# Layer 0's mix: products with h in plain fp32, four column blocks accumulated at once over all K, and no weight splits on GpSimd

## The chip, the core and the metric

The kernel runs on one NeuronCore of a Trainium2 chip. TensorE (PE in the profile) does matrix products into PSUM, VectorE (DVE) and ScalarE (ACT) do elementwise work, GpSimd (POOL) does elementwise work in SBUF, and SyncE (SP) issues DMA transfers from HBM. Each engine works through its own queue in order; semaphores join them. The metric is the device time of one execution in microseconds (us).

## What is computed

The reference is a two-layer decoder trunk for 256 tokens of width 2048, in float32. Only layer 0's mix is touched by the change:

```python
mod = cond @ w_ada[layer] + b_ada[layer]          # six vectors of 2048 for each layer
h = rmsnorm(x, g_pre_mix[layer]) * (1 + sc_m) + sh_m
z = h @ w_in_ab[i]                                # 2048 -> 5408 columns
y_a = chunked_spatial_gating(z[..., :2 * A_WIDTH], ...)
y_b = rwkv7_time_mix(z[..., 2 * A_WIDTH:], ...)
y = jnp.concatenate([y_a, y_b], axis=-1) @ w_out_ab[i]
x = x + gt_m * rmsnorm(y, g_post_mix[layer])
```

Behind it come layer 0's SwiGLU FFN, layer 1's attention, and layer 1's FFN. The conditioning matrix `w_ada` is 201 MB in all; shift and scale of layer 0's mix (33.5 MB of it) are needed before h exists, the other ten vectors are needed later.

## The kernel before, in words

**Products.** Every large product goes through the same scheme. Activations lie transposed in SBUF, 16 K-tiles of 128 rows by 256 tokens. A chunk is a weight tile of 256 rows of K by 512 columns (512 KB), loaded by SP into `w32` (four buffers). `load_split` (L187) makes two fp32r tiles of it: `wh`, a rounded copy by ACT (L193), and `wl`, the remainder `w32 - wh`, by DVE or, every `Split.every`-th time, by GpSimd (L194 to L196). The activation is split the same way, into h and l. A product of one K-tile and one token tile is then three fp32r matmuls, h wh + h wl + l wh (`mm_chunk`, L207 to L209). `dense` (L221) runs one block of 512 columns over all of K in two PSUM banks of the pool `ps_mm` (four banks; the pool `ps_ms` has the other four, for everything small).

**Start of layer 0.** `strips(kt)` (L425) loads two 1 MB strips of `w_ada` into four slots, takes their dot products with the conditioning vector on DVE (`ada_dot`, L115), and makes K-tile kt of h: `h32` on DVE (L437), its rounded copy `H0` on ACT (L438) and the remainder `L0` on DVE (L439). Since K-tiles become ready one by one, the first seven column blocks (`first`: lora of 288 columns, then k0, k1, r0, r1, v0, v1 of 512) are run in four groups of four K-tiles. For each group and block, two PSUM banks are filled with four K-tiles (`group_block` and `mm_group`, L456 to L458) and added to an SBUF tile (`acc`: a copy by ACT for the first group at L464, an add by DVE at L466 after that).

**The background program.** `rk_gen` (L502 to L902) is the RWKV-7 part: token shift, decay, keys, scores of 64-token chunks, inverses of triangular blocks (L670 to L719, mostly DVE), the chain over four chunks (L721 to L890, small fp32 matmuls), group norm and `YB`. It is a generator that yields a cost at each step. After each weight chunk `pump` (L164) adds credit (`Bg.rate`, 1.8 a chunk and 3 from the chain on) and takes steps of it for that credit. The yields add up to about 121: lora and decay 14.3, keys 17.9, r, bonus and v 16, scores 8, inverses 31.8, chain and norms 33. It waits for blocks that are not yet in the set `have`. `pump` also takes steps of `ada_gen` (L118), each a 512 KB load of `w_ada` and a dot product on DVE; its rate is 1 a chunk, and 2.2 from the chain on.

**Order of layer 0.** First the four groups, where the background program runs beside the last (`last_group`, L910, 14 chunks); then four `dense` blocks of the gMLP part (`evac_av` and `evac_au`, 32 chunks); then the half of w_out that reads `YA` (L994, 16 chunks), with what is left of the background program; then the half that reads `YB` (L1024, 16 chunks), and `residual_norm`. A scheduler of the framework orders instructions within the queues, so that neighbouring steps may change places.

Of the kernel before, what the change touches and what calls it, by code (L numbers as in the profile page):

```python
# [14 lines left out]
P = 128  # L15
# [7 lines left out]
GROUPS = (4, 4, 4, 4)  # L23
# [29 lines left out]
def trunk(ctx: ExitStack, tc, io, out, dbg=None):  # L53
# [12 lines left out]

    cols = cpool.tile([P, NCOL], F32, name="cols")
# [31 lines left out]
    cond = cpool.tile([P, D], F32, name="cond")  # L99
    A.dma_start(cond, io["c"].to_broadcast([P, D]))  # L100
# [82 lines left out]
    class Split:  # L183
        n = 0
        every = 0

    def load_split(src, ncol):  # L187
        w32 = wpool.tile([P, 2, 512], F32, tag="w32", name="w32", bufs=4)
        SY.dma_start(w32[:, :, :ncol], src)  # L189
        wh = wpool.tile([P, 2, 512], F32R, tag="wh", name="wh", bufs=3)  # L190
        wl = wpool.tile([P, 2, 512], F32R, tag="wl", name="wl", bufs=3)
        with tc.high_priority(PRI):
            A.activation(wh[:, :, :ncol], w32[:, :, :ncol], AF.Copy)  # L193
            Split.n += 1  # L194
            eng = G if Split.every and Split.n % Split.every == 0 else V
            eng.tensor_sub(wl[:, :, :ncol], w32[:, :, :ncol], wh[:, :, :ncol].bitcast(F32))  # L196
        return wh, wl
# [13 lines left out]
    class Late:  # L211
        """steps of an evacuation that wait for the next block's first chunks"""
# [73 lines left out]
    def residual_norm(X, U, st, layer, which, Ht, Lt, base=None):  # L286
# [4 lines left out]
        # mean (x + r u)^2 from the sums, then its root  # L291
# [77 lines left out]
    # =================== layer 0 mix ===================  # L369
    xT = hpool.tile([P, KT, S], F32, tag="X", name="xT")  # L370
    A.dma_start(xT, io["xT"])
    H0 = new_hT("H0", "hT0")
    L0 = new_hT("H1", "hT0l")
    hx, lx = hl(H0, L0)

# [16 lines left out]
    slots = [KBf[:, 0:D], KBf[:, D:2 * D], SCf[:, 0:D], SCf[:, D:2 * D]]  # L392
# [3 lines left out]
    vAf = vA.rearrange("p t n -> p (t n)")  # L396

# [12 lines left out]
    with tc.tile_pool(name="spool", bufs=1) as sp:  # L410
        # 1 / rms of every token, on all partitions
        sq = RA.rearrange("p x g s -> p (x g) s")
# [8 lines left out]
        V.reciprocal(rbc, rbc)  # L421

        ns = [0]

        def strips(kt):  # L425
            cc = sp.tile([P, 2], F32, tag="cc", name="cc", bufs=3)
            for s_ in range(2):
                w = slots[ns[0] % 4]
                ns[0] += 1
                SY.dma_start(w, io["w_ada"][0, s_, kt])  # L430
                ada_dot(w, 0, D, cc[:, s_:s_ + 1])
            V.tensor_add(cc[:, 0:1], cc[:, 0:1], col("b_ada", kt))
            V.tensor_scalar(cc[:, 1:2], cc[:, 1:2], col("b_ada", KT + kt), 1.0, op0=OP.add,
                            op1=OP.add)
            V.tensor_mul(cc[:, 1:2], cc[:, 1:2], col("g_pre_mix", kt))
            h32 = sp.tile([P, S], F32, tag="h32", name="h32", bufs=2)
            V.scalar_tensor_tensor(h32, xT[:, kt, :], cc[:, 1:2], rbc, op0=OP.mult, op1=OP.mult)  # L437
            A.activation(H0[:, kt, :], h32, AF.Identity, bias=cc[:, 0:1])  # L438
            V.scalar_tensor_tensor(L0[:, kt, :], h32, cc[:, 0:1], H0[:, kt, :].bitcast(F32),  # L439
                                   op0=OP.add, op1=OP.subtract)  # L440

        def group_block(src, ncol, k0, n):
            ps = [ps_mm.tile([P, 512], F32, name="mm") for _ in range(NT)]
            for c in range(n // 2):
                wh, wl = load_split(src(k0 // 2 + c), ncol)
                mm_group(ps, c, k0, wh, wl, ncol, n)
                yield ps

        def mm_group(ps, c, k0, wh, wl, ncol, n):
            for k in range(2):  # L450
                j = 2 * c + k
                kt = k0 + j
                for t in range(NT):
                    o = ps[t][:, :ncol]
                    h, l = hx(kt, t), lx(kt, t)
                    T.matmul(o, h, wh[:, k, :ncol], start=(j == 0), stop=False)  # L456
                    T.matmul(o, h, wl[:, k, :ncol], start=False, stop=False)  # L457
                    T.matmul(o, l, wh[:, k, :ncol], start=False, stop=(j == n - 1))  # L458

        def acc(nm, ps, ncol, gi):  # L460
            z = zn_tiles[nm]
            for t in range(NT):
                if gi == 0:
                    A.activation(z[:, t, :ncol], ps[t][:, :ncol], AF.Copy)  # L464
                else:
                    V.tensor_tensor(z[:, t, :ncol], z[:, t, :ncol], ps[t][:, :ncol], op=OP.add)  # L466

        Split.every = 3
        k0 = 0
        for kt in range(GROUPS[0]):  # L470
            strips(kt)
        nk = GROUPS[0]
        for gi, n in enumerate(GROUPS[:-1]):
            nxt = GROUPS[gi + 1]
            done, slot, total = 0, 0, len(first) * n // 2
            for nm, src, ncol in first:
                for ps in group_block(src, ncol, k0, n):
                    slot += 1
                    while done < nxt and done * total < slot * nxt:
                        strips(nk)  # L480
                        nk += 1
                        done += 1
                acc(nm, ps, ncol, gi)
            k0 += n
    dump("h", H0)
    A.dma_start(indT, io["indT"])

    def head_bcast(out, g, rows):
        """rows of heads 2g, 2g+1 onto their 64 partitions each"""
        T.matmul(out, indT[:, g, :], rows, start=True, stop=True)  # L490
# [3 lines left out]
    E = hpool.tile([P, 2, 8, S], F32, tag="X", name="E")  # L494
    have = set()
# [6 lines left out]
    def rk_gen():  # L502
        # lora
# [78 lines left out]
        # kk  # L582
# [22 lines left out]
        # k' and b  # L605
# [31 lines left out]
        # causal scores of every chunk: strict against the removal keys, full against r  # L637
        Bg.rate = 1.8
        SRA = hpool.tile([P, 64, 64], F32, tag="X", name="SRA")
# [29 lines left out]
        # inverse of the 32 x 32 diagonal blocks  # L669
        Ada.rate, Split.every = 1, 2  # L670
# [50 lines left out]
        # chain over the chunks  # L721
        Bg.rate = 3
        Ada.rate, Split.every = 2.2, 3
# [63 lines left out]
        def group_norm(ts, gw):  # L787
            """y = (y - mean) rstd G1 + B1 for a range of tokens, gw pairs of heads at a time"""
# [106 lines left out]
        YB = hpool.tile([P, 2, 8, S], F32R, tag="X", name="YB")  # L895
# [12 lines left out]
    Split.every = 2  # L908

    def last_group():  # L910
        n = GROUPS[-1]
        k0 = KT - n
        for nm, src, ncol in first:
            for ps in group_block(src, ncol, k0, n):
                pump(AR, BR)
            acc(nm, ps, ncol, len(GROUPS) - 1)
            have.add(nm)

    last_group()
# [6 lines left out]
    # A: gelu, layernorm of v  # L926
# [6 lines left out]
    for b in range(2):  # L933
        dense(lambda ch, b=b: win[6 + b, ch], KT, hx, lx, 512, evac_av(b), AR, BR)
# [37 lines left out]
    for b in range(2):  # L972
        dense(lambda ch, b=b: win[8 + b, ch], KT, hx, lx, 512, evac_au(b), AR, BR)
    YA = hpool.tile([P, 2, 8, S], F32R, tag="H1", name="YA")
# [27 lines left out]
    Split.every = 3  # L1002
# [28 lines left out]
    Split.every = 0  # L1031
# [4 lines left out]
    # =================== FFN ===================  # L1036
# [53 lines left out]
    # =================== layer 1 attention ===================  # L1090
# [117 lines left out]
def _layout(inputs):  # L1208
# [24 lines left out]
    def tiled(w, cols_list):  # L1233
        """[K, N] -> [blocks, K/256, 128, 2, width]"""
# [70 lines left out]
```

## Time and profile before

| | us |
|---|---|
| median of 3 runs (lowest, highest) | 2599.43 (2598.14, 2600.51) |
| the profiled execution, span | 2604.5 |
| layer 0's mix in it, to the last product with YB | 641.7 |
| PE busy, whole span | 2415.6 |
| DVE busy, whole span | 1770.2 |
| POOL busy, whole span | 235.9 |

The profiled execution is the only one with a trace, and its span is its own time; it is 5.1 us (0.2%) longer than the median. In the views by stretch, each row gives a stretch of the span, the busy time of each engine with its number of instructions, the granted TensorE clock as a share of full speed, the busy share of the DMA engines, and the bytes that they moved. A busy time joins instructions that overlap.

### The profile page before, as it was taken

The page shows a single profiled execution, that of the slowest core. Times are in us where ns is not written, and L with a number is a line of the kernel's source. Part 1 is how long each engine was busy: PE and PEld are TensorE (multiplying, and loading weights), DVE is VectorE, ACT ScalarE, POOL GpSimd, SP SyncE. Part 2 cuts the span into 40 slices and gives each one's busy share as a digit, 9 for nine tenths or more (in the row PEclk, how much of TensorE's full clock was granted, in tenths as well). Part 3 has the DMA queues.
Part 4 walks back from the last instruction along what each step waited for, and adds up shares of the span by engine and source line. Part 5 has one row for each costly group of instructions (what it writes and reads, how often), then busy time and mean ns, then how long its engine had stood idle before and what let it go on. Part 6 is the DMA issues. An engine that isn't in the chain of part 4 may idle for free. (4 is left out here: it accounts for less than half of the span.)

```text
span 2604.5 us, 30648 instructions
## 1 busy us (share of the span) xinstructions
PE 2415.6 (93%) x11296; PEld 1944.2 (75%) x11296; DVE 1770.2 (68%) x2318; ACT 1115.7 (43%) x1508; POOL 235.9 (9%) x131
## 2 busy tenths in 40 slices
PE   4888887997999999999998999999999999999998
PEld 3666666855778777788887777877777888888886
DVE  6998999468777777754545788786777545444444
ACT  3436332435544434444444444445644444443443
POOL 1222752002100000000000010000100000000000
PEclk8999898879999999999999999999999999999999
DMA  9867665458689888755555788886587555556554
GB/s 364 323 256 271 207 211 202 155 163 287 212 308 318 311 299 303 276 190 204 192 194 170 251 306 307 298 305 237 180 312 279 191 187 191 187 188 209 192 190 152
DMA packets 167126, 623.55 MB, mean 239 GB/s; under 512 B 18512, under 2 KB 20752, under 8 KB 161856
## 3 DMA queue, kind: packets, MB, share of 16 engines
q1 hardware_dynamic: 165312, 612.74, 67.4%
q10 hardware_dynamic: 1664, 8.86, 0.9%
q8 instruction: 88, 1.44, 0.2%
q14 instruction: 62, 0.51, 0.1%
HBM read 619.39 MB, written 2.13 MB: 239 GB/s over the span
## 5 line engine op out<-in xcount | busy, mean ns | idle before, releaser
L193 ACT ACTIVATE wh<-w 128x1024 fp32r<-128x1024 f32 (+1 forms) x776 | 817.8, 1055 | 1107.6 <-PE mm L209 1000.2
L196 DVE TENSOR_TENSOR wl<-w,wh 128x1024 fp32r<-128x1024 f32 (+1 forms) x728 | 896.3, 1238 | 520.5 <-ACT wh L193 519.6
L208 PE MATMUL mm<-wl,hF 128*128 128x512 f32 x1408 | 554.5, 394 | 18.0 <-DVE wl L196 17.4
L115 DVE SCALAR_TENSOR_TENSOR ada<-ada,cond 128x1024 f32<-128x1024 f32 x320 | 417.2, 1306 | 220.8 <-DMA ada<-in_w_ada_dram 219.8
L207 PE MATMUL mm<-wh,hF 128*128 128x512 f32 x1408 | 553.1, 393 | 0.0
L209 PE MATMUL mm<-wh,hFl 128*128 128x512 f32 x1408 | 550.4, 391 | 0.0
L208 PEld LDWEIGHTS mm<-wl,hF 128*128 128x128 f32 x1408 | 264.5, 188 | 90.2 <-DVE wl L196 37.2
L207 PEld LDWEIGHTS mm<-wh,hF 128*128 128x128 f32 x1408 | 264.6, 188 | 54.2
L209 PEld LDWEIGHTS mm<-wh,hFl 128*128 128x128 f32 x1408 | 264.5, 188 | 53.8
L209 PE MATMUL mm<-wh,aL 128*128 128x512 f32 x704 | 277.7, 394 | 0.0
L208 PE MATMUL mm<-wl,aH 128*128 128x512 f32 x704 | 276.2, 392 | 0.0
L207 PE MATMUL mm<-wh,aH 128*128 128x512 f32 x704 | 273.4, 388 | 0.0
L196 POOL TENSOR_TENSOR wl<-w,wh 128x1024 fp32r<-128x1024 f32 (+1 forms) x48 | 127.7, 2661 | 443.3 <-ACT wh L193 433.2
L207 PE MATMUL mm<-wh,hA 128*128 128x512 f32 x384 | 156.7, 408 | 0.0
L208 PEld LDWEIGHTS mm<-wl,aH 128*128 128x128 f32 x704 | 132.2, 188 | 30.8
L208 PE MATMUL mm<-wl,hA 128*128 128x512 f32 x384 | 153.5, 400 | 1.9 <-DVE wl L196 1.8
L207 PEld LDWEIGHTS mm<-wh,aH 128*128 128x128 f32 x704 | 132.2, 188 | 29.3
L209 PE MATMUL mm<-wh,hAl 128*128 128x512 f32 x384 | 152.1, 396 | 0.0
L209 PEld LDWEIGHTS mm<-wh,aL 128*128 128x128 f32 x704 | 132.5, 188 | 26.1
L457 PE MATMUL mm<-wl,hT 128*128 128x512 f32 (+1 forms) x224 | 91.8, 410 | 33.5 <-DVE wl L196 28.7
L1126 POOL TENSOR_SCALAR dh<-cst 128x384 f32<-128x384 f32 x16 | 29.6, 1851 | 1026.6 <-PE mm L209 745.2
L456 PE MATMUL mm<-wh,hT 128*128 128x512 f32 (+1 forms) x224 | 88.4, 404 | 14.2 <-ACT hT L438 12.9
(310 smaller groups left out, 2611.6 us busy)
## 6 DMA issues: line engine op xcount, KB each, us to landing
w<-in_w_ffn_in_dram SPq DMA_DIRECT2D x352, 512.0 KB, 4.0
ada<-in_w_ada_dram SPq DMA_DIRECT2D x320, 512.0 KB, 5.2
w<-in_w_ffn_out_dram SPq DMA_DIRECT2D x176, 512.0 KB, 4.2
w<-in_w_qkv_dram SPq DMA_DIRECT2D x96, 512.0 KB, 5.0
w<-in_w_in_dram SPq DMA_DIRECT2D x80, 512.0 KB, 4.5
KB<-in_w_ada_dram SPq DMA_DIRECT2D x16, 1024.0 KB, 7.5
SCN<-in_w_ada_dram SPq DMA_DIRECT2D x16, 1024.0 KB, 6.6
w<-in_w_out_dram SPq DMA_DIRECT2D x32, 512.0 KB, 4.7
```

Source lines behind the costliest of these rows:

```text
L115: V.scalar_tensor_tensor(w, w, 1.0, cond[:, k0:k0 + n], op0=OP.mult, op1=OP.mult, accum_out=dst)
L193: A.activation(wh[:, :, :ncol], w32[:, :, :ncol], AF.Copy)
L196: eng.tensor_sub(wl[:, :, :ncol], w32[:, :, :ncol], wh[:, :, :ncol].bitcast(F32))
L207: T.matmul(o, h, wh[:, k, :ncol], start=(kt == 0), stop=False)
L208: T.matmul(o, h, wl[:, k, :ncol], start=False, stop=False)
L209: T.matmul(o, l, wh[:, k, :ncol], start=False, stop=(kt == nkt - 1))
L456: T.matmul(o, h, wh[:, k, :ncol], start=(j == 0), stop=False)
L457: T.matmul(o, h, wl[:, k, :ncol], start=False, stop=False)
L1126: G.tensor_scalar(dh, alibi, slope, None, op0=OP.mult)
```

## The change

The products with h (the seven blocks and the four gMLP blocks, eleven in all) are done on fp32 operands directly, with one `matmul` call in place of three. Their weights are used as loaded; h is one fp32 tile, made in place in `xT` by one ACT instruction a K-tile, after DVE has multiplied `xT` by 1/rms once. Lora, k0, k1 and r0 are accumulated side by side in eight PSUM banks, over all of K, as the strips come in two K-tiles at a time; r1, v0, v1 and the gMLP blocks follow through a new `dense32`. The strips have six slots in place of four, and the weights of the first four blocks go to two sets of slots in tiles that are still unused. The loads of the conditioning vector and of x are issued first, x in four pieces. `Split` is gone: where weights are still split (w_out, FFN, attention), DVE makes `wl` each time. `E`, `SRA`, `YB` and `YA` change places in SBUF. Outside layer 0's mix and `load_split` the program is the same.

```diff
+    cond = cpool.tile([P, D], F32, name="cond")
+    A.dma_start(cond, io["c"].to_broadcast([P, D]))
+    xT = hpool.tile([P, KT, S], F32, tag="X", name="xT")
+    for k4 in range(4):
+        A.dma_start(xT[:, 4 * k4:4 * k4 + 4, :], io["xT"][:, 4 * k4:4 * k4 + 4, :])
...
-            Split.n += 1
-            eng = G if Split.every and Split.n % Split.every == 0 else V
-            eng.tensor_sub(wl[:, :, :ncol], w32[:, :, :ncol], wh[:, :, :ncol].bitcast(F32))
+            V.tensor_sub(wl[:, :, :ncol], w32[:, :, :ncol], wh[:, :, :ncol].bitcast(F32))
...
+    slots = [KBf[:, 0:D], KBf[:, D:2 * D], SCf[:, 0:D], SCf[:, D:2 * D], EXf[:, 0:D],
+             EXf[:, D:2 * D]]
...
+    wslots = [[RAf[:, i * 1024:(i + 1) * 1024] for i in range(4)],
+              [f[:, i * 1024:(i + 1) * 1024] for f in (vAf, VTf) for i in range(2)]]
...
+        def strips(j):
+            cc = sp.tile([P, 2, 2], F32, tag="cc", name="cc", bufs=3)
             for k in range(2):
...
+                for s_ in range(2):
+                    w = slots[ns[0] % len(slots)]
+                    ns[0] += 1
+                    SY.dma_start(w, io["w_ada"][0, s_, 2 * j + k])
+                    ada_dot(w, 0, D, cc[:, s_, k:k + 1])
+            V.tensor_tensor(cc, cc, bada[:, :, 2 * j:2 * j + 2], op=OP.add)
+            V.scalar_tensor_tensor(cc[:, 1, :], cc[:, 1, :], 1.0, col("g_pre_mix", 2 * j, 2),
+                                   op0=OP.add, op1=OP.mult)
+            return cc
+
+        def h_rows(j, cc):
+            for k in range(2):
+                kt = 2 * j + k
+                A.activation(xT[:, kt, :], xT[:, kt, :], AF.Identity, bias=cc[:, 0, k:k + 1],
+                             scale=cc[:, 1, k:k + 1])
...
+        acc = {"lora": [bank(ps_ms, "ms") for _ in range(NT)],
+               "k0": [bank(ps_mm, "mm") for _ in range(NT)],
+               "k1": [bank(ps_mm, "mm") for _ in range(NT)],
+               "r0": [bank(ps_ms, "ms") for _ in range(NT)]}
+        for j in range(KT // 2):
+            cc = strips(j)
+            if j == 0:
+                for k4 in range(4):
+                    ks = slice(4 * k4, 4 * k4 + 4)
+                    V.tensor_tensor(xT[:, ks, :], xT[:, ks, :], rb4, op=OP.mult)
+            h_rows(j, cc)
+            for i, (nm, src, ncol) in enumerate(first[:4]):
+                w = wslots[j % 2][i][:, :2 * ncol].rearrange("p (k n) -> p k n", k=2)
+                SY.dma_start(w, src(j))
+                for k in range(2):
+                    kt = 2 * j + k
+                    for t in range(NT):
+                        T.matmul(acc[nm][t][:, :ncol], xT[:, kt, tsl(t)], w[:, k, :],
+                                 start=(kt == 0), stop=(kt == KT - 1))
+        for nm, src, ncol in first[:4]:
+            for t in range(NT):
+                A.activation(zn_tiles[nm][:, t, :ncol], acc[nm][t][:, :ncol], AF.Copy)
...
+    have = {"lora", "k0", "k1", "r0"}
...
+    def dense32(wsrc, evac):
+        ps = [ps_mm.tile([P, 512], F32, name="mm") for _ in range(NT)]
+        for ch in range(KT // 2):
+            w = wpool.tile([P, 2, 512], F32, tag="w32", name="w32", bufs=4)
+            SY.dma_start(w, wsrc(ch))
+            for k in range(2):
+                kt = 2 * ch + k
+                for t in range(NT):
+                    T.matmul(ps[t], xT[:, kt, tsl(t)], w[:, k, :], start=(kt == 0),
+                             stop=(kt == KT - 1))
+            pump(AR, BR)
+        evac(ps)
...
+    for nm, src, ncol in first[4:]:
+        dense32(src, evac_z(nm))
...
-        dense(lambda ch, b=b: win[6 + b, ch], KT, hx, lx, 512, evac_av(b), AR, BR)
+        dense32(lambda ch, b=b: win[6 + b, ch], evac_av(b))
...
-        dense(lambda ch, b=b: win[8 + b, ch], KT, hx, lx, 512, evac_au(b), AR, BR)
+        dense32(lambda ch, b=b: win[8 + b, ch], evac_au(b))
```

The lines that are taken out beside these are the old `strips`, `group_block`, `mm_group`, `acc` and `last_group`, told above.

More of the change, by code (lines that the diff above doesn't have):

```diff
@@ L22 @@
 S = 256
-GROUPS = (4, 4, 4, 4)
 POOLQ = (3,)
@@ L98, in trunk @@
     V.memset(eps_l, LN_EPS)
-    cond = cpool.tile([P, D], F32, name="cond")
-    A.dma_start(cond, io["c"].to_broadcast([P, D]))
     A.activation(cond, cond, AF.Silu)
@@ L180, in pump @@
                 Bg.credit -= c
-    class Split:
-        n = 0
-        every = 0
     def load_split(src, ncol):
@@ L367, in split_from @@
         V.tensor_sub(l_ap, ps_ap, h_ap.bitcast(F32))
[L370 to L374, printed above, removed]
+    EX = hpool.tile([P, KT, S], F32, tag="H0", name="EX")
+    sq = hpool.tile([P, KT, S], F32, tag="H1", name="sq")
     lpool_cm = tc.tile_pool(name="lpool", bufs=1)
@@ L391, in trunk @@
     SCf = SCN.rearrange("p a b -> p (a b)")
-    slots = [KBf[:, 0:D], KBf[:, D:2 * D], SCf[:, 0:D], SCf[:, D:2 * D]]
+    EXf = EX.rearrange("p k s -> p (k s)")
+    slots = [KBf[:, 0:D], KBf[:, D:2 * D], SCf[:, 0:D], SCf[:, D:2 * D], EXf[:, 0:D],
+             EXf[:, D:2 * D]]
     RAf = RA.rearrange("p x g s -> p (x g s)")
@@ L410, in trunk @@
     with tc.tile_pool(name="spool", bufs=1) as sp:
-        sq = RA.rearrange("p x g s -> p (x g) s")
         pss = msbank()
@@ L421, in trunk @@
         V.reciprocal(rbc, rbc)
+        rb4 = rbc.rearrange("p (o s) -> p o s", o=1).to_broadcast([P, 4, S])
+        a0 = COLS["b_ada"][0]
+        bada = cols[:, a0:a0 + 2 * KT].rearrange("p (s k) -> p s k", s=2)
         ns = [0]
[L425 to L449, printed above, removed]
-            for k in range(2):
[L451 to L458, printed above, removed]
@@ L460, in acc @@
-        def acc(nm, ps, ncol, gi):
-            z = zn_tiles[nm]
-            for t in range(NT):
[L463 to L484, printed above, removed]
@@ L485, in trunk @@
-    dump("h", H0)
+        def strips(j):
+            cc = sp.tile([P, 2, 2], F32, tag="cc", name="cc", bufs=3)
+            for k in range(2):
+                for s_ in range(2):
[7 more added lines that the diff above has]
+            return cc
@@ new lines, in h_rows, with bank @@
+        def h_rows(j, cc):
[3 more added lines that the diff above has]
+                             scale=cc[:, 1, k:k + 1])
+        def bank(pool, nm):
+            return pool.tile([P, 512], F32, name=nm)
+        acc = {"lora": [bank(ps_ms, "ms") for _ in range(NT)],
+               "k0": [bank(ps_mm, "mm") for _ in range(NT)],
+               "k1": [bank(ps_mm, "mm") for _ in range(NT)],
+               "r0": [bank(ps_ms, "ms") for _ in range(NT)]}
@@ L493, in trunk @@
     A.dma_start(w2a2, io["w2a2"])
-    E = hpool.tile([P, 2, 8, S], F32, tag="X", name="E")
-    have = set()
+    E = hpool.tile([P, 2, 8, S], F32, tag="H0", name="E")
+    have = {"lora", "k0", "k1", "r0"}
     pp_cm = tc.tile_pool(name="pp", bufs=1)
@@ L638, in rk_gen @@
         Bg.rate = 1.8
-        SRA = hpool.tile([P, 64, 64], F32, tag="X", name="SRA")
+        SRA = hpool.tile([P, 64, 64], F32, tag="H1", name="SRA")
         mk = cn("mask").rearrange("p (r t) -> p r t", r=2)
@@ L668, in rk_gen @@
         pp_cm.__exit__(None, None, None)
-        Ada.rate, Split.every = 1, 2
+        Ada.rate = 1
         kp = rk["kp_cm"].__enter__()
@@ L722, in rk_gen @@
         Bg.rate = 3
-        Ada.rate, Split.every = 2.2, 3
+        Ada.rate = 2.2
         Sst = kp.tile([P, 8, 64], F32, name="Sst")
@@ L894, in rk_gen @@
         yield from group_norm(slice(192, 256), 8)
-        YB = hpool.tile([P, 2, 8, S], F32R, tag="X", name="YB")
+        YB = hpool.tile([P, 2, 8, S], F32R, tag="H1", name="YB")
         rk["YB"] = YB
@@ L906, in trunk, with evac_z, f @@
     Bg.rate = 1.8
[L908 to L916, printed above, removed]
+    def dense32(wsrc, evac):
[10 more added lines that the diff above has]
+        evac(ps)
+    def evac_z(nm):
+        def f(ps):
+            for t in range(NT):
+                A.activation(zn_tiles[nm][:, t, :], ps[t], AF.Copy)
             have.add(nm)
-    last_group()
+        return f
+    for nm, src, ncol in first[4:]:
+        dense32(src, evac_z(nm))
     wsT = lp.tile([P, 8, P], F32, tag="b4", name="wsT")
@@ L972, in trunk @@
     for b in range(2):
-        dense(lambda ch, b=b: win[8 + b, ch], KT, hx, lx, 512, evac_au(b), AR, BR)
-    YA = hpool.tile([P, 2, 8, S], F32R, tag="H1", name="YA")
+        dense32(lambda ch, b=b: win[8 + b, ch], evac_au(b))
+    YA = hpool.tile([P, 2, 8, S], F32R, tag="X", name="YA")
     for k2 in range(4):
@@ L1001, in trunk @@
     YB = rk["YB"]
-    Split.every = 3
     Ada.rate = None
@@ L1030, in trunk @@
     hF = [new_hT("H0", "hF0"), new_hT("H1", "hFl0")]
-    Split.every = 0
     residual_norm(X, YP, st, 0, "ffn", hF[0], hF[1], base=x0)
```

## Prediction

> **What bounds the kernel now.** I read the page first, then a table by stretch, then the same table for some tiles, then groups of instructions.
>
> ```profile
> span 2604.5 us, 30648 instructions
> PE 2415.6 (93%) x11296; PEld 1944.2 (75%) x11296; DVE 1770.2 (68%) x2318; ACT 1115.7 (43%) x1508; POOL 235.9 (9%) x131
> ```
>
> PE seems to bound everything. The stretches say otherwise for the first quarter:
>
> ```profile
> core 0: us, PE busy (x) PEld busy (x) DVE busy (x) ACT busy (x) POOL busy (x), PEclk, DMA share, GB/s
> 0.00:42.00 42.00, 8.73 (x33) 7.13 (x33) 20.50 (x32) 11.50 (x13) 3.56 (x6) 0.95 0.95 372
> 42.00:188.00 146.00, 116.34 (x479) 92.84 (x480) 135.67 (x172) 52.19 (x68) 33.31 (x12) 0.92 0.80 302
> 188.00:256.00 68.00, 59.18 (x265) 45.56 (x264) 59.93 (x85) 42.23 (x71) 22.45 (x11) 0.95 0.75 266
> 256.00:413.00 157.00, 134.37 (x596) 102.70 (x595) 155.70 (x230) 54.28 (x77) 91.04 (x52) 0.89 0.65 215
> 413.00:584.00 171.00, 155.21 (x1340) 117.18 (x1338) 107.06 (x165) 61.51 (x96) 14.30 (x6) 0.83 0.49 164
> 584.00:641.70 57.70, 48.58 (x192) 37.70 (x192) 47.67 (x63) 31.39 (x63) 13.80 (x5) 0.94 0.83 285
> 665.00:2604.00 1939.00, 1884.00 (x8354) 1533.40 (x8352) 1222.18 (x1533) 853.17 (x1102) 53.27 (x37) 0.99 0.69 240
> ```
>
> The rows are: start, three groups of the split products, the last group, the gMLP blocks, w_out's half with YA, w_out's half with YB, and all that follows layer 0's mix. Loads bound the first row (DMA share 0.95). DVE is busy 93% of the second and 99% of the fourth. PE is the bound in the fifth and in the last. After the mix the change does nothing: `Split.every` was 0 there, so DVE made every split already, PE is busy 97%, and conditioning steps that come earlier only leave DVE, at 63%, freer. So 1963 us (2604.5 - 641.7, the 23 us of the norm among them) stay, and the forecast is about the first 641.7.
>
> **The price of a product.** A split product is three fp32r matmuls; a plain one shows as two instructions (16 calls at L527 gave 32 records, x12 of them in a run below; the last row gives one record's length).
>
> ```profile
> 1504.70 0.39 PE L208 MATMUL mm<-wl,hA 128*128 128x512 f32 x1
> ...
> 1506.29 0.39 PE L209 MATMUL mm<-wh,hAl 128*128 128x512 f32 x1
> ```
> ```profile
> 207.96 2.75 PE L527 MATMUL ms<-tz,w2a 128*128 128x256 f32 x12
> ```
> ```profile
> L527 PE MATMUL ms<-tz,w2a 128*128 128x256 f32 x32 | 7.6, 379 | 0.0
> ```
>
> Seven steps of the fp32r stream take 1.59 us, 0.227 each, so a split product costs 0.681. In the fp32 run, (2.75 - 0.379) / 11 = 0.2155 us a step for 256 columns, so 0.431 for 512, and two of them, 0.862, a product (0.485 for lora's 288 columns). On 320 products of 512 columns PE pays 320 x 0.181 = 58 us more. What DVE is spared:
>
> ```profile
> L196 DVE TENSOR_TENSOR wl<-w,wh 128x1024 fp32r<-128x1024 f32 x68 | 94.6, 1394 | 8.6 <-ACT wh L193 8.6
> L115 DVE SCALAR_TENSOR_TENSOR ada<-ada,cond 128x1024 f32<-128x1024 f32 x92 | 138.2, 1508 | 25.5 <-DMA ada<-in_w_ada_dram 25.4
> L115 DVE SCALAR_TENSOR_TENSOR KB<-KB,cond 128x2048 f32<-128x2048 f32 x16 | 36.5, 2284 | 10.5 <-ACT cond L101 10.5
> L439 DVE SCALAR_TENSOR_TENSOR hT0l<-h,cc,hT 128x256 fp32r<-128x256 f32 x16 | 11.9, 746 | 1.2 <-ACT hT L438 1.2
> L437 DVE SCALAR_TENSOR_TENSOR h<-xT,cc,rbc 128x256 f32<-128x256 f32 x16 | 7.7, 483 | 0.4
> ```
> ```profile
> L196 DVE TENSOR_TENSOR wl<-w,wh 128x1024 fp32r<-128x1024 f32 x136 | 163.2, 1221 | 4.9 <-ACT wh L193 4.9
> L115 DVE SCALAR_TENSOR_TENSOR ada<-ada,cond 128x1024 f32<-128x1024 f32 x97 | 118.8, 1225 | 98.3 <-DMA ada<-in_w_ada_dram 98.0
> L115 DVE DVE_READ_ACCUMULATOR ada<-ada,cond 128x1 f32 x97 | 8.0, 83 | 0.0
> ```
>
> The first fence is 0 to 640 us, the second a stretch of layer 0's FFN (700 to 1100), where GpSimd splits nothing: the same split takes 1.22 instead of 1.39 us there, and a conditioning step 1.31 with its readout. I use the second prices, since GpSimd splits nothing after the change.
>
> **Start, part by part.** The loads are, from the shapes, 32 strips of 1.049 MB, 8 x (0.295 + 3 x 0.524) MB of weights, and 4.6 MB of x, conditioning vector, columns and constants: 53.0 MB. At the 372 GB/s of the first row that is 142 us, over at 144 with 2 us allowed for the first landing. DVE's share is 32 x 2.3 = 74 us and some 15 of small steps and the four multiplications by 1/rms; PE's is 8 bursts of 12 x 0.862 + 4 x 0.485 = 12.3 us, 98 in all, each beside the next pair's 5.9 MB (16 us). So loads bound it. Six strip slots and two sets of weight slots keep SP's queue ahead of what it waits for: a strip's slot comes free by a 2.3 us dot of the sixth strip before, a weight slot by the burst of two pairs before. Should SP wait for a slot, the weights and the r1 loads stand behind it in its queue, and PE waits for them; should ACT's h rows wait for DVE's dots, PE waits too, with nothing else behind them on ACT. The eighth bank is the one that the sum of squares had; it is free before the first h row, since that needs 1/rms. The last weights take 5 us behind the last strip (1.87 MB); strip at 139, dot, small steps and h rows 4 us, burst 12.3: the start ends at **155**. That the vector and x come first hides under it: DVE's first dot waits less, but DVE is not late. Bounds: 150 if the burst follows the weights closely, 165 if the loads keep 345 GB/s. A rule speaks against this. The Trainium skill, page "TensorE: Matmul & The Clock Gate", Part 1, says that an idle window of about 3.4 us halves PE's clock until a busy one has passed; with pauses of 4 us between bursts, each burst would by it be an estimated 1.7 us longer, the start would end at 157 and the time would be 2579. The second row's granted 0.92, with PE busy 80% in bursts, shows that some clock is lost in this way, and no size.
>
> Before, at 188 us, all strips and three quarters of seven blocks were done; now, at 155, all strips and four whole blocks. The remaining seven blocks are 56 chunks of 4 products, 3.45 us of PE each. Evacuating the eight banks is ACT's, beside k1's and r0's last products.
>
> **From 155 to YB, by sections of the background program.** Its own work is taken from the stretches in which it ran before; rows for all instructions, for those on `ms` banks (its PE work), for conditioning steps, and for `wl`:
>
> ```profile
> 200.00:369.00 169.00, 146.40 (x651) 110.17 (x650) 161.59 (x229) 78.88 (x128) 93.31 (x54) 0.90 0.66 223
> 369.00:466.00 97.00, 78.61 (x525) 63.80 (x525) 90.87 (x142) 30.95 (x38) 22.09 (x9) 0.85 0.63 214
> 466.00:584.00 118.00, 111.74 (x963) 81.25 (x961) 59.17 (x93) 44.45 (x73) 7.13 (x3) 0.85 0.47 153
> ```
> ```profile
> 200.00:369.00 169.00, 43.58 (x262) 30.95 (x261) 23.57 (x63) 21.57 (x53) 0.90 0.66 223
> 369.00:466.00 97.00, 18.52 (x302) 17.34 (x303) 7.99 (x20) 6.40 (x11) 0.85 0.63 214
> 466.00:584.00 118.00, 84.46 (x865) 62.27 (x863) 10.60 (x17) 24.50 (x43) 0.85 0.47 153
> ```
> ```profile
> 200.00:369.00 169.00, 60.57 (x68) 0.90 0.66 223
> 369.00:466.00 97.00, 24.48 (x40) 0.85 0.63 214
> ```
> ```profile
> 200.00:369.00 169.00, 55.72 (x129) 27.50 (x130) 26.84 (x16) 44.13 (x17) 0.90 0.66 223
> 369.00:466.00 97.00, 33.03 (x74) 15.71 (x74) 14.51 (x12) 21.70 (x8) 0.85 0.63 214
> ```
> ```profile
> 188.00:256.00 68.00, 9.90 (x16) 0.95 0.75 266
> ```
>
> (The last is the adds into z, L466, which go.) A section's chunks are its yields over the rate.
>
> - Lora to scores: 56.2 / 1.8 = 31 chunks. PE 31 x 3.45 + 43.6 = 151. DVE 161.6 - 60.6 - 26.8 - 9.9 + 31 x 1.31 = 105. PE bounds it: 151, and 9 for waits where PE's queue stands behind a token shift or a product that DVE has not finished. 160.
> - Inverses: 31.8 / 1.8 = 18 chunks. PE 62 + 18.5 = 81, DVE 90.9 - 24.5 - 14.5 + 18 x 1.31 = 75. The two are near each other, and PE's small matmuls come after DVE's loop: 88.
> - Chain: 33 / 3 = 11 chunks, 7 plain at 3.45 and 4 of w_out at 12 x 0.227 = 2.72. PE 35 + 84.5 = 120, as before (118), when 13 chunks of w_out lay there.
> - Rest of w_out's half: 12 chunks, PE 33. With 2.2 conditioning steps a chunk they load 12 x 3.2 x 0.524 = 20 MB, 54 us at 372 GB/s, but the chain moves only 153 GB/s and can take some of it: 44.
>
> That is 412, of it 384 PE's own and 28 for waits and clock; YB's products can start at 567, where they started at 584. **w_out's half with YB:** PE 43.6; its splits and conditioning steps were
>
> ```profile
> 584.00:641.70 57.70, 26.77 (x64) 12.92 (x64) 13.85 (x10) 13.80 (x5) 0.94 0.83 285
> ```
> ```profile
> 584.00:641.70 57.70, 18.87 (x24) 0.94 0.83 285
> ```
>
> DVE's 47.67 loses 13.85 for ten splits, gains 16 x 1.22, as it takes over GpSimd's, and loses 3 as twelve steps go from 1.57 to 1.31: 50. I take 52 for 57.7; ten splits on DVE, five of GpSimd's and what was made early make the sixteen. The end is at 619 against 641.7, **23 us less**: 2581.8 of a profiled 2604.5. The median is 5.1 below the profiled span, so 2577 in its terms. ACT's 88 rounded copies go too, at no price: ACT is under 65% busy in every row.
>
> **Rivals.**
>
> Better overlap. If the sections overlap fully, only PE's 384 count, and YB's half takes 48: 155 + 384 + 48 = 587, 55 less, 2545. For it: DVE was kept at 99% when it was the bound. Against it: PE's queue is in order, and the background's matmuls wait for DVE within it.
>
> PE's clock, to the slower side. Before, a low clock cost nothing while DVE was late; now PE is the bound, with 236 us of weight products (56 x 3.45 + 16 x 2.72). At 0.83 of the clock, the fifth row's, they take 285; with the waits kept the end is at 668, 26 more, 2626. It decides from a clock of 0.91 down, where 23 us are lost. For it: from 256 to 584 the rows have 0.89 and 0.83. Against: those rows had PE waiting, or tiny matmuls, and the last row, a dense stream, has 0.99. By the page named above a gate needs an idle window, which a dense stream does not leave.
>
> Loads in the start. With the 302 GB/s of the second row the start ends 33 us later, at 188, and the whole is 10 slower: 2609. The gain is gone at 320 GB/s. Against: in that row SP waited for slots behind a DVE that was 93% busy, and now DVE has half of the start free.
>
> That a plain product is cheaper than 0.862 (not all of the passes done) is excluded by L527's records as far as 256 columns go.
>
> **How the numbers follow.** A measurement of this kernel tells about 0.2%, 5 us, from no change. The forecast has 0.57, better overlap 0.14, the clock 0.14, late loads 0.07; 0.08 is left for sums that end near nothing. Of the forecast's share all but 0.01 is faster by over 5 us: faster 0.70; same 0.10, with what of the clock and load cases stops halfway; slower 0.20. The range reaches to the whole of better overlap, 2545, and on the other side past late loads to 2612, short of the full clock case.
>
> **What would show it.** In the profile after: 640 plain products of 512 columns' records at 0.43 us a step; the eight-bank products over at about 155 us with DMA share above 0.9 until 140; no `wl` on POOL; DVE below 80% from 155 to the scores and PE above 90%; products with YB from about 567 to 619; 665 us onwards unchanged in length. It would be wrong if the start ends after 170, if PE idles over 12% between start and YB, or if its granted clock there is under 0.9.

## The result and the profile after

The changed kernel takes 2560.2 us in the median (2554.26 to 2565.03, 4 runs), the kernel before 2599.97 beside it: a ratio of 0.9839, 95% interval 0.9818 to 0.9861, some 40 us less. Measured again in another session the ratio was 0.9819 (0.9801 to 0.9836). The forecast was 2577, 22 less, with a range from 2545 to 2612.

Its page begins:

```profile
span 2555.7 us, 29570 instructions
## 1 busy us (share of the span) xinstructions
PE 2429.3 (95%) x10944; PEld 1860.5 (73%) x10944; DVE 1619.6 (63%) x2176; ACT 1037.1 (41%) x1423; POOL 102.0 (4%) x83
```

PE has more to do than before (2429 against 2416 us busy), DVE 151 us less and POOL 134 less, in a span that is 48.8 shorter. That is 9 more than the medians differ: the traced execution before lies above its median, the one after below. The table by stretch, cut where the steps of the prediction end (columns as before):

```profile
core 0: us, PE busy (x) PEld busy (x) DVE busy (x) ACT busy (x) POOL busy (x), PEclk, DMA share, GB/s
0.00:146.60 146.60, 110.05 (x288) 57.44 (x289) 85.46 (x98) 21.50 (x31) 1.24 (x6) 0.94 0.98 392
146.60:312.50 165.90, 156.22 (x512) 77.66 (x510) 110.62 (x215) 49.53 (x94) 29.63 (x31) 0.95 0.76 259
312.50:405.00 92.50, 78.62 (x414) 40.28 (x415) 78.29 (x143) 12.80 (x20) 13.65 (x6) 0.91 0.70 235
405.00:508.00 103.00, 102.75 (x906) 67.71 (x904) 51.84 (x92) 37.41 (x64) 0.00 (x0) 0.92 0.58 191
508.00:563.60 55.60, 51.95 (x248) 41.61 (x244) 40.55 (x57) 22.08 (x28) 0.00 (x0) 0.94 0.76 263
563.60:607.30 43.70, 43.70 (x194) 35.90 (x192) 30.41 (x41) 31.23 (x60) 0.00 (x0) 1.00 0.62 217
607.30:620.40 13.10, 4.92 (x26) 4.11 (x25) 12.60 (x23) 6.32 (x18) 3.48 (x2) 0.74 0.23 81
620.40:2555.70 1935.30, 1881.13 (x8377) 1535.84 (x8375) 1209.85 (x1513) 856.24 (x1110) 54.04 (x38) 0.99 0.68 236
```

The rows are the start, lora to scores, the inverses, the chain, the rest of w_out's half with YA, its half with YB, the gap before the FFN's first product, and all that follows. From the start to YB the bound has moved: PE is busy 389.5 of 417 us there (93%), DVE 281 (67%); before, DVE was busy 99% of the gMLP stretch. The same kernel traced a second time took 410.4 us there, PE busy 384.9, so single stretches are told to some 7 us. The layer's mix, to YB's last product, ends at 607.3 instead of 641.7.

The price of a plain product is read from a group and from one unbroken run of the stream, both of the changed kernel:

```profile
L901 PE MATMUL mm<-w,xT 128*128 128x512 f32 x448 | 216.3, 630 | 4.6 <-DMA w<-in_w_in_dram 4.6
```
```profile
339.61 7.89 PE L901 MATMUL mm<-w,xT 128*128 128x512 f32 x18
```

The 224 calls left 448 records, two a product. The mean of 630 ns holds some longer records, up to 1222; the median record is 592 ns long, and (7.89 - 0.592) / 17 = 0.429 us a step, so 0.859 a product, where 0.862 was worked out from 256-column records.

Where the two traces differ, in us (the stretches before are 0 to 584.1, 584.1 to 641.7, 641.7 to 660.7 and the rest of the span):

| | before | after | difference | forecast |
|---|---|---|---|---|
| start of the products with YB | 584.1 | 563.6 | -20.5 | -17 |
| products with YB | 57.6 | 43.7 | -13.9 | -5.7 |
| their end to the FFN's first product | 19.0 | 13.1 | -5.9 | 0 |
| from there to the end | 1943.8 | 1935.3 | -8.5 | 0 |

What the second and third lines have in common shows in the table of conditioning steps alone (DVE's instructions on `ada`, two for each step), first before, then after:

```profile
584.00:641.70 57.70, 18.87 (x24) 0.94 0.83 285
641.70:660.70 19.00, 4.84 (x8) 0.64 0.44 157
```
```profile
508.00:563.60 55.60, 13.23 (x22) 0.94 0.76 263
563.60:607.30 43.70, 0.00 (x0) 1.00 0.62 217
607.30:620.40 13.10, 0.00 (x0) 0.74 0.23 81
```

Before, twelve steps fell beside the products with YB and four into the norm behind them, which needs their vector. After, none did: 111 had been taken by then. PE is busy without a gap in that half (43.70 of 43.70). The theory that I set out to test: DVE bounded the mix; relieved of the splits it lets PE run up to its own limit, and it also takes conditioning steps early, which is where 14 unforecast us lie (19.8 less in the second and third lines, where 5.7 were forecast). The rival: GpSimd's splits were what made the half with YB slow, and their removal mended it.

The theory passes over a third cause, the program's own order. `pump` places one conditioning step a call, and 2.2 once the chain has begun. Before, it is called 62 times ahead of the products with YB and the chain begins in the 51st call: 51 + 11 x 2.2 = 75 steps. The norm needs 96; twelve more are placed among the products with YB, and `need(0, 4)` puts the last nine behind their third block (neighbouring steps change places, so in the trace 80 had run when the half began). After, r1, v0 and v1 run through `dense32` and pump too: 72 calls, the chain from the 49th, 49 + 23 x 2.2 = 99 steps ahead of the half, and nothing is left for `need` to force. Which of the two causes moved the steps is read from the runs below.

### The profile page after: what moved, and what is told of

It is laid out like the page before. It is cut to its first block, busy times and chain, and to the rows that moved or that the text cites. A ratio compares the mean times of both kernels' runs of the same rounds, so it can differ in the third digit from the quotient of the medians.

```text
span 2555.7 us, 29570 instructions
## 1 busy us (share of the span) xinstructions
PE 2429.3 (95%) x10944; PEld 1860.5 (73%) x10944; DVE 1619.6 (63%) x2176; ACT 1037.1 (41%) x1423; POOL 102.0 (4%) x83
## 5 line engine op out<-in xcount | busy, mean ns | idle before, releaser
L192 DVE TENSOR_TENSOR wl<-w,wh 128x1024 fp32r<-128x1024 f32 x688 | 836.8, 1223 | 532.9 <-ACT wh L191 531.7
L191 ACT ACTIVATE wh<-w 128x1024 fp32r<-128x1024 f32 x688 | 728.3, 1059 | 1005.4 <-PE mm L205 941.7
L117 DVE SCALAR_TENSOR_TENSOR ada<-ada,cond 128x1024 f32<-128x1024 f32 x320 | 392.9, 1229 | 286.1 <-DMA ada<-in_w_ada_dram 285.2
L901 PE MATMUL mm<-w,xT 128*128 128x512 f32 x448 | 216.3, 630 | 4.6 <-DMA w<-in_w_in_dram 4.6
L901 PEld LDWEIGHTS mm<-w,xT 128*128 128x128 f32 x448 | 86.2, 201 | 105.9 <-issue 97.7
L204 PEld LDWEIGHTS mm<-wl,hA 128*128 128x128 f32 x384 | 72.8, 190 | 20.1 <-DVE wl L192 6.3
L205 PEld LDWEIGHTS mm<-wh,hAl 128*128 128x128 f32 x384 | 72.7, 189 | 15.1
```

The lines of the kernel that those rows point to most:

```text
L117: V.scalar_tensor_tensor(w, w, 1.0, cond[:, k0:k0 + n], op0=OP.mult, op1=OP.mult, accum_out=dst)
L192: V.tensor_sub(wl[:, :, :ncol], w32[:, :, :ncol], wh[:, :, :ncol].bitcast(F32))
L205: T.matmul(o, l, wh[:, k, :ncol], start=False, stop=(kt == nkt - 1))
L901: T.matmul(ps[t], xT[:, kt, tsl(t)], w[:, k, :], start=(kt == 0), stop=(kt == KT - 1))
```

## The experiments

All ratios are to the kernel before, run on the same chip in the same session, with 95% intervals. There are eleven runs.

**No splits on GpSimd, in the kernel before.** One part of the change alone:

```diff
-            eng = G if Split.every and Split.n % Split.every == 0 else V
+            eng = V
```

> The kernel before with every wl made by DVE, none by GpSimd. Theory (DVE bounds the mix before): DVE takes over 47 splits at 1.22 us (57 us) and gets back 68 x 0.17 + 92 x 0.28 = 37 us, as its splits and conditioning steps are no longer stretched, so the mix ends 10 to 25 us later and the time is 2610 to 2625. Rival (GpSimd's splits were themselves the loss, by contention and by PE waiting for 2.66 us splits): the mix ends earlier, 2580 to 2592, and the half of w_out with YB takes under 50 us instead of 57.6.

Measured: 0.9934 (0.9916 to 0.9952), 17 us faster in the ratio. I had expected it slower; the rival's sign was right, but not its place. The half with YB took 50.9 us (57.6 before), yet the gap behind it grew to 22.7, so the two together fell only from 76.6 to 73.6. The rest of the gain came earlier: w_out's products began at 397.6 instead of 416.0, though of these 18 us only 6 were left when the products with YB began (578.3 for 584.1). This trace shows 10 us less than the one before in all; it is of one of the two slowest of the six executions (2580.4 to 2596.3). The engines up to w_out's first product and up to YB's, each time before and in this run:

```profile
0.00:416.00 416.00, 321.38 (x1391) 250.74 (x1391) 374.80 (x519) 162.44 (x230) 151.82 (x81) 0.92 0.75 269
```
```profile
0.00:397.60 397.60, 325.51 (x1391) 251.44 (x1391) 345.15 (x536) 161.90 (x229) 50.78 (x43) 0.91 0.77 274
```
```profile
0.00:584.10 584.10, 473.86 (x2706) 365.42 (x2706) 478.89 (x681) 221.81 (x322) 164.65 (x86) 0.89 0.67 239
0.00:578.30 578.30, 481.52 (x2705) 370.07 (x2705) 458.81 (x726) 222.30 (x322) 50.78 (x43) 0.87 0.70 243
```

To w_out's first product DVE is busy 30 us less, but it had also taken fewer conditioning steps by then (44, not 48). By YB's first product the steps are level (81 or 82, and 80), and DVE is busy 20 us less with over 40 more splits to make. Two instructions of the inverses say why, one with two SBUF inputs (L688) and one with a single input (L681). In the kernel before, DVE's and GpSimd's timeline at one place, and the group L681:

```profile
398.21 2.51 DVE L688 TENSOR_TENSOR AT<-AT,KBn 128x247 f32<-128x247 f32 x1
398.01 2.43 POOL L196 TENSOR_TENSOR wl<-w,wh 128x1024 fp32r<-128x1024 f32 x1 [8.82 <-ACT wh L193]
```
```profile
L681 DVE STREAM_TRANSPOSE AT<-SCN 32x1024 f32<-32x1024 f32 x4 | 8.0, 1988 | 0.1
```

The same two in this run:

```profile
L688 DVE TENSOR_TENSOR AT<-AT,KBn 128x247 f32<-128x247 f32 x2 | 0.8, 404 | 0.0
L681 DVE STREAM_TRANSPOSE AT<-SCN 32x1024 f32<-32x1024 f32 x4 | 7.9, 1967 | 0.1
```

A two-input instruction of 0.40 us took 2.51 beside a split on GpSimd, and ended 0.28 us behind that split. All 31 of L688 took 21.3 us before and 10.4 in this run. The transposes took the same in both, though two of the four ran beside a split. The Trainium skill says it so, page "SBUF — State Buffer", section "SBUF: two separate sides": GpSimd, reading SBUF, and a VectorE instruction with two SBUF inputs take a shared port pair by an exclusive lock for the whole instruction, and whichever comes second blocks. The trace agrees: the 2.1 us lost by that instruction are nearly the 2.23 us that the split, begun 0.20 us earlier, still had to run.

**No wl for the products with h, in the kernel before.** DVE's relief without PE's price. `load_split` returns `wh` in the place of `wl`, so the product h wl is computed as h wh once more:

```diff
             A.activation(wh[:, :, :ncol], w32[:, :, :ncol], AF.Copy)
+            if not lo:
+                return wh, wh
```

> The kernel before, where the eleven blocks of products with h make no wl: wh is used in its place, so that part of the computation (h wl) is replaced by another product of the same cost. PE keeps three fp32r matmuls a product, ACT its rounded copies; DVE and GpSimd lose 88 splits. Theory (DVE bounds the mix): DVE loses about 73 splits less 13 of w_out, 60 x 1.39 = 83, and contention; the mix ends 60 to 90 us earlier, 2510 to 2540, below the changed kernel's 2560 by PE's price of 58 us less what its start gained. Rival (the gain of the change is from its start, the eight banks and the loads): 2585 to 2598.

Measured: 0.9687 (0.967 to 0.9704), 82 us faster, 2522 in its own median, inside what the theory gave. To the first w_out product, and from there to the first with YB:

```profile
0.00:355.10 355.10, 304.22 (x1391) 242.29 (x1392) 271.29 (x502) 164.49 (x232) 48.79 (x44) 0.94 0.88 324
355.10:498.00 142.90, 137.63 (x1316) 104.78 (x1316) 89.06 (x130) 58.58 (x92) 14.46 (x6) 0.93 0.52 173
```

With the same number of matmuls as before (1391), PE now is busy 86% of the first stretch, where it had been 77%. So DVE and GpSimd's remainders cost the kernel before some 82 us, and the changed kernel keeps about half of that; PE's 58 us for plain products are the likely rest, though the starts differ too.

This run also tells the two causes of the early steps apart. DVE is relieved here as in the changed kernel, at 62% in the second row, but the program's order is still the old one, 75 steps ahead of the half with YB. The conditioning steps from the first product with YB to the FFN's first:

```profile
498.00:574.30 76.30, 21.74 (x30) 0.84 0.73 254
```

Fifteen steps fall there, and the stretch takes 76.3 us, as in the kernel before (76.6). So room on DVE alone does not move the steps; it fits that the changed program places 24 more of them ahead of the half. No run has the changed kernel with the old placing and nothing else; the next run but one comes near it.

**GpSimd splitting again, in the changed kernel.** Every third `wl` of w_out:

```diff
-            V.tensor_sub(wl[:, :, :ncol], w32[:, :, :ncol], wh[:, :, :ncol].bitcast(F32))
+            Split.n += 1
+            eng = G if Split.every and Split.n % Split.every == 0 else V
+            eng.tensor_sub(wl[:, :, :ncol], w32[:, :, :ncol], wh[:, :, :ncol].bitcast(F32))
```

> The changed kernel with GpSimd making every third wl of w_out again (10 of 32). Theory (the half with YB is short because conditioning steps ran ahead and DVE is free there): a GpSimd split takes 2.7 instead of 1.2 us, and PE waits for some of them; the half with YB takes 44 to 48 us instead of 43.7, the gap to the FFN stays at 13, the time is 2558 to 2566. Rival (it is short because GpSimd splits nothing): the half takes 53 to 58, the gap 15 to 19, the time is 2570 to 2580.

Measured: 0.9825 (0.981 to 0.9839), not to be told from the changed kernel. The half with YB and the gap:

```profile
560.60:604.30 43.70, 43.70 (x194) 35.89 (x192) 30.38 (x37) 30.48 (x59) 10.76 (x5) 1.00 0.64 215
604.30:617.50 13.20, 5.11 (x26) 4.27 (x25) 12.69 (x23) 6.81 (x18) 3.48 (x2) 0.74 0.25 90
```

POOL is busy 10.76 us with five splits and PE does not lose a tenth of a microsecond. The rival falls for this stretch. Taken with the first experiment: GpSimd's splits cost where DVE is the bound, and nothing that can be seen in this half, where DVE has room.

**Sixteen conditioning steps held back, in the changed kernel.** Steps 80 to 95 wait for the first YB block, by a factor 1.0 that is made from its row sums:

```diff
+            if b == 0:
+                Ada.one = cpool.tile([P, 1], F32, name="one_late")
+                V.tensor_scalar(Ada.one, st[:, 0, 0, 0:1], 0.0, 1.0, op0=OP.mult, op1=OP.add)
```

> The changed kernel with conditioning steps 80 to 95 held until the first YB block is evacuated (they use a 1.0 made from its row sums), which is how many fell there before. Theory (steps that ran ahead made the half with YB and the norm short): the stretch from the first YB product to the first FFN product takes 68 to 77 us instead of 56.8, YB's products start 0 to 5 us earlier, the time is 2568 to 2580. Rival (GpSimd's splits made it long before): the stretch stays at 55 to 60 and the time at 2553 to 2563.

Measured: 0.9911 (0.9897 to 0.9925), 2580.4, against 0.9825 for the run beside it: half of the gain is gone. The stretches (YB's half, the gap), and the steps in them:

```profile
558.60:609.50 50.90, 46.54 (x194) 36.80 (x192) 40.83 (x60) 30.95 (x59) 0.00 (x0) 0.97 0.77 262
609.50:634.30 24.80, 5.25 (x25) 4.30 (x25) 21.32 (x39) 6.95 (x18) 3.48 (x2) 0.66 0.55 183
```
```profile
558.60:609.50 50.90, 12.89 (x20) 0.97 0.77 262
609.50:634.30 24.80, 7.71 (x12) 0.66 0.55 183
```

75.7 us from the first YB product to the FFN's first, where the changed kernel has 56.8 and the kernel before 76.6, with no split on GpSimd. Ten steps (two instructions each) fall beside the products and six behind them. The hold is stricter than the old order was, since no held step can run before the first YB block is done; that late steps cost the 20 us is shown all the same. In DVE's timeline of this run the norm's wait is seen directly: a dot that waits for its load, and the evacuation of YB queued behind it.

```profile
613.50 1.28 DVE L117 SCALAR_TENSOR_TENSOR ada<-ada,one_late,cond 128x1024 f32<-128x1024 f32 x1
614.70 0.08 DVE L117 DVE_READ_ACCUMULATOR ada<-ada,one_late,cond 128x1 f32 x1
617.66 1.28 DVE L117 SCALAR_TENSOR_TENSOR ada<-ada,one_late,cond 128x1024 f32<-128x1024 f32 x1 [2.88 <-DMA ada<-in_w_ada_dram]
618.87 0.08 DVE L117 DVE_READ_ACCUMULATOR ada<-ada,one_late,cond 128x1 f32 x1
618.87 1.29 DVE L261 TENSOR_TENSOR YP<-YP,gtg 128x512 f32<-128x512 f32 x2
```

**Half of the plain products, in the changed kernel.** The second K-tile of each of the 56 chunks is left out:

```diff
-            for k in range(2):
+            for k in range(1):
```

> The changed kernel with the second K-tile of each of the 56 plain chunks left out (half of their products; the loads stay). PE has 96 us less from the first plain chunk to the first YB product, 417 us after the change. Theory (PE bounds most of this stretch, DVE the inverses): it shortens by 45 to 80 us. Rival (DVE, or the background program's chain of waits, bounds it): it shortens by less than 25 us.

Measured, in a single execution: YB's products start at 495.2 instead of 563.6, 68 us earlier, so PE does bound most of that stretch. But the time is 2530.6, only some 30 less than the changed kernel's. The half with YB and the gap show where the rest went, all instructions and then the conditioning steps:

```profile
495.20:556.50 61.30, 49.99 (x194) 36.94 (x192) 50.97 (x81) 30.97 (x59) 0.00 (x0) 0.92 0.90 308
556.50:588.80 32.30, 4.86 (x22) 4.02 (x21) 23.85 (x41) 7.40 (x18) 4.77 (x2) 0.55 0.75 245
```
```profile
495.20:556.50 61.30, 23.09 (x38) 0.92 0.90 308
556.50:588.80 32.30, 12.73 (x20) 0.55 0.75 245
```

The program's order is that of the changed kernel, 99 steps ahead of the half, but with less time on PE only 82 had run by then, and 29 fell into the 93.6 us that had been 56.8. The 37 us lost there are more than half of what PE gave. So the early steps of the changed kernel need both, a place ahead in the program and the time to run.

**No more than 96 steps before the norm, in the changed kernel.**

```diff
+        if Ada.n == Ada.cap:
+            return
```

> The changed kernel with no conditioning step beyond the 96 that layer 0's norm needs until that norm (after the change 111 were done before the first YB product; the 15 others go to the FFN). Theory (w_out's half with YA is held up by DVE and loads of conditioning steps: 56 us from 508 to 563.6 for what is 33 us of PE): YB's products start 5 to 12 us earlier, the stretch to the first FFN product stays at 57, the time is 2548 to 2556. Rival (PE and the waits for the background program hold it): it moves by less than 3 us, 2557 to 2563.

Measured: 0.9833 (0.9814 to 0.9852): no change that can be told. The place was right: from the first product with YA to the first with YB it takes 55.4 us, PE busy throughout, where the changed kernel took 62.2, and 61.3 in its second trace. The start of YB's products is less clear: 557.9 here, but 563.6 and 556.7 in the two traces of the changed kernel.

```profile
502.50:557.90 55.40, 55.24 (x314) 44.65 (x313) 33.45 (x44) 24.52 (x32) 0.00 (x0) 1.00 0.50 171
```
```profile
1700.00:1812.20 112.20, 12.27 (x20) 0.95 0.65 218
```

The second fence is the conditioning steps alone, in layer 1's w_o and the norm behind it: ten of the steps that were put off fell there (none in the changed kernel), and that stretch took 112.2 us instead of 107.2. What is saved in one place is paid in the other, 5 us of it as far as these rows show.

**The start: columns first.** In the changed kernel DVE's first dot began at 23.9 us (17.4 before), behind two small steps that waited for the columns:

```diff
+    cols = cpool.tile([P, NCOL], F32, name="cols")
+    A.dma_start(cols, io["cols"])
     cond = cpool.tile([P, D], F32, name="cond")
     A.dma_start(cond, io["c"].to_broadcast([P, D]))
...
     A.activation(cond, cond, AF.Silu)
+    A.dma_start(cst, io["consts"])
```

> The changed kernel with the 205 KB of columns loaded first and the constants issued behind the Silu. In the changed kernel DVE's first conditioning dot began at 23.9 us, behind two small steps that waited for the columns, and PE's first burst at 43; from there PE was busy 101 of 104 us. Theory (PE bounds the start from its first burst on): dots begin at 13 to 17, the first burst at 33 to 37, the first plain chunk (146.6 after the change) starts 5 to 9 us earlier, the time is 2550 to 2556. Rival (the loads bound the start's end, at a DMA share of 0.98): the first plain chunk moves by less than 3 us, the time stays at 2557 to 2563.

Measured: 0.9841 (0.9825 to 0.9856), no change. Dots began at 13.6, but the first burst stayed at 42.2 and the first plain chunk at 146.4, so this run tells neither side from the other. DVE's timeline of this run:

```profile
31.48 2.29 DVE L117 SCALAR_TENSOR_TENSOR EX<-EX,cond 128x2048 f32<-128x2048 f32 x1 [8.60 <-DMA EX<-in_w_ada_dram]
33.70 0.08 DVE L117 DVE_READ_ACCUMULATOR EX<-EX,cond 128x1 f32 x1
34.28 2.29 DVE L117 SCALAR_TENSOR_TENSOR EX<-EX,cond 128x2048 f32<-128x2048 f32 x1 [0.51 <-DMA EX<-in_w_ada_dram]
36.50 0.08 DVE L117 DVE_READ_ACCUMULATOR EX<-EX,cond 128x1 f32 x1
36.50 1.75 DVE L418 RECIPROCAL rbc<-rbc 128x256 f32<-128x256 f32 x1
```

1/rms, which the first burst needs, stands in the queue behind two dots of the second pair, and those wait 8.6 us for their strips. Both edits together, columns first and the cap of 96:

> Both of the two edits before, columns first and the cap of 96. If they act at different places, as both theories say, their gains add: 10 to 20 us less than the changed kernel, 2541 to 2550. If only one of them does anything, the time is that one's.

Measured: 0.983 (0.9808 to 0.9853). Neither edit does anything that can be told, nor do both.

**The start: 1/rms ahead of the second pair.** The second pair's dots take their factor 1.0 from the multiplied x, which puts them behind it; with columns first, and with the changed kernel's own loads; and the changed kernel again beside them.

```diff
+                V.tensor_scalar(one1, xT[:, KT - 1, 0:1], 0.0, 1.0, op0=OP.mult, op1=OP.add)
...
-                    ada_dot(w, 0, D, cc[:, s_, k:k + 1])
+                    ada_dot(w, 0, D, cc[:, s_, k:k + 1], one1 if j == 1 else 1.0)
```

> The kernel with columns first, and in addition 1/rms and the multiplication of x placed ahead of the second pair's dots in DVE's queue (those dots take their factor 1.0 from the multiplied x). With columns first alone, DVE had the first pair's dots done at 22.5 us, but then stood 8.6 us for the second pair's strips, and the first burst stayed at 42.2. Theory (PE, busy 101 of 104 us behind its first burst, bounds the start): the first burst comes at 33 to 37, the first plain chunk at 137 to 142 instead of 146.6, the time is 3 to 9 us below the changed kernel's. Rival (the loads, at a share of 0.98, bound the end of the start): PE waits for weights between bursts, and the first plain chunk stays within 3 us of 146.6.

> The changed kernel with its own order of loads (conditioning vector and x, then columns), and 1/rms placed ahead of the second pair's dots as in the run beside it. DVE's first dot stays at 23.9, behind the steps that wait for the columns. Theory (first burst sets the start's end, PE bound): the burst comes at 39 to 42, the first plain chunk at 143 to 146, the time within 4 us of the changed kernel's. Rival (columns do not matter once 1/rms is placed right): the same as the run beside it.

> The changed kernel again, on the chip of the two runs beside it, for comparison: 2554 to 2565, the first plain chunk at 146 to 147, 56 to 58 us from the first YB product to the first FFN product.

Measured: 0.9821 (0.9808 to 0.9835), 0.9825 (0.9797 to 0.9853) and 0.9819 (0.9801 to 0.9836). PE's timeline in the first of these runs, and in the changed kernel:

```profile
31.15 3.73 PE L468 MATMUL ms<-RA,xT 128*128 128x288 f32 x8 [4.25 <-ACT xT L444]
...
143.66 3.60 PE L904 MATMUL mm<-w,xT 128*128 128x512 f32 x8
```
```profile
43.05 4.21 PE L465 MATMUL ms<-RA,xT 128*128 128x288 f32 x8 [17.06 <-ACT xT L442]
...
146.65 2.74 PE L901 MATMUL mm<-w,xT 128*128 128x512 f32 x6
```

The first burst came 12 us earlier and the first plain chunk 3 (with the old loads 36.7 and 145.2). So my theory that PE bounds the start falls but for 3 us: that PE was busy 101 of 104 us only says that the late burst had used up its slack. With an early burst PE waits for rows of h again, and the loads bound the end of the start, at a share of 0.98 and more; in the changed kernel PE ends 3 us behind that limit. Nothing of the 3 us is seen later: the products with YB began at 557.3, and at 556.7 in the changed kernel run beside it. None of these versions beats the changed kernel by more than the interval.

## Why the prediction was right, and where it was off

The direction held, and so did the mechanism forecast for the mix, DVE relieved and PE the bound. The gain was 40 us for 22, and it lies within the range by luck: the range reached down to 2545 for better overlap of the sections, which did not come, and what made the time shorter was not among the rivals. Step by step:

- **The price of a plain product**, two instructions of 0.43 us for 512 columns, was right to a half per cent.
- **The start** was forecast to end at 155 by loads and ended at 146.6: the loads' limit is near 143.7, as the run with the early burst showed, and PE's late first burst adds 3. The mis-sized term is the rate: 392 GB/s over the whole start instead of 372. I wrote that DVE's first dot waits less when the vector and x come first; it came 6.5 us later (23.9 for 17.4), behind the columns. That, and 1/rms queued behind the second pair's dots, hid but for those 3 us.
- **From the start to YB** I gave 412 us, 384 of it PE's; it took 417, with PE busy 389.5. By sections: 166 for 160, 92.5 for 88, then 158.6 for 164 over the chain and the rest (the cut between these two lies elsewhere, as only one chunk of w_out fell into the chain). The second trace took 410.4, so the sum was right and the sections are within the scatter. Halving the plain products moved YB's start by 68 of 96 us, which fits a stretch bound by PE outside the inverses.
- **w_out's half with YB, 52 us, and the norm behind it, unchanged.** This is where the forecast was 14 us short: 56.8 us measured for 71. I kept twelve conditioning steps in this half, and carried the norm's wait along with the 1963 us that stay. My own sections say otherwise: 31 + 18 chunks at one step and 7 + 16 at 2.2 place 99 steps ahead of the half, and the norm needs 96; before, it was 75. The runs that held sixteen back (75.7 us) and that lost steps by a shorter stretch (93.6) show that late steps are what these 20 us cost. That it is not DVE's room alone shows in the run without `wl`, where DVE was free, the placing old and the stretch 76.3.
- **GpSimd.** I priced its splits by two groups, 0.17 and 0.28 us on a split and a dot. In the kernel before they cost more: without them it was 17 us faster, where those prices had it 20 slower. Each short two-input step of the background program could be held up as well, as L688 was. For the forecast this mattered little, as DVE is no longer the bound.
- **The rivals.** The clock was granted at 0.91 to 0.95 from the start to YB, near the point from which I had it decide, but PE's shortfall was 27.5 us of 417 in all, within the 28 that I had allowed, and its busy time 389.5 for 384. The pauses of 4 us between bursts did not come: behind its first burst PE was idle for 3 us of 104. Loads in the start were faster, not slower. Better overlap did not come about: PE idled those 27.5 us, and the mix ended at 607.3, not 587.
- **After the norm** the profiled execution is 8.5 us shorter. Of that 2.7 are in layer 1's w_o and norm, where eleven conditioning steps fell before and none now. The rest is not told from scatter: from the FFN's first product to the end, 1943.8 before and 1935.3 after, it took 1936.0 in the second trace of the changed kernel and 1937.6 to 1947.2 in five of its variants, with the same steps left to take.

## What to carry to other kernels

Before a matmul is made dearer to spare another engine, look in which stretch that engine is the bound: here plain fp32 costs PE 58 us and still wins, as DVE was 99% busy there. Work that a program paces by its chunks, like the conditioning steps, moves when a change adds chunks that pace it, so the change is also felt in stretches that it does not touch; count the steps again, and ask whether there is time for them to run where they are placed. Handing two-input elementwise work to GpSimd beside a busy VectorE can cost more than it takes off.

## What the hardware showed that I had not expected

A short two-input VectorE instruction went from 0.40 to 2.51 us beside a split on GpSimd, and the whole kernel became 0.7% faster when VectorE did all of GpSimd's splits itself. Loads ran at 392 GB/s for 147 us, at a DMA share of 0.98. The clock was granted at 0.92 in the chain's 103 us though PE was busy for all but 0.25 us of them, with small matmuls among the products. The Trainium skill's rule on the page "TensorE: Matmul & The Clock Gate", Part 1, by which the gate closes after an idle window of about 3.4 us, does not say why: no such pause is in that row.
